# Constant products in TensorE's waits while two norms finish, and the first two weight pieces behind each norm multiplied pass by pass

## The chip, the core and the metric

The kernel runs on one NeuronCore of one Trainium2 chip. The metric is the device time of one execution in microseconds (us); lower is better. Times of whole kernels are given as the median of several executions. One execution was also taken by the hardware profiler; its rows are what the prediction reads.

## The reference

A trunk of two layers over 256 tokens of width 1024, all in float32. The lines that matter for this change are the norms with their scale and shift, and the dense matrix products right behind two of them:

```python
def rmsnorm(x, g):
    xf = x.astype(jnp.float32)
    y = xf * lax.rsqrt(jnp.mean(xf * xf, axis=-1, keepdims=True) + EPS)
    return (y * g.astype(jnp.float32)).astype(x.dtype)
...
    for l in range(DEPTH):
        if l == N_A:
            hn_kv = modulate(rmsnorm(h, kv_norm_g), kv_sh, kv_sc)
            shared = fox_shared_kv(hn_kv, fox_w_kv, fox_w_f, fox_b_f)
        a = modulate(rmsnorm(h, norm_g[l, 0]), sh1, sc1)
        if l < N_A:
            mix = retention(a, ret_w_in[l], ret_w_o[l])
        else:
            mix = forgetting_attention(a, fox_w_qg[j], fox_w_o[j], shared[0], shared[1], shared[2])
        h = h + g1[:, None, :] * mix
        m = modulate(rmsnorm(h, norm_g[l, 1]), sh2, sc2)
        if l % 2 == 0:
            ff = swiglu(m, ffn_w_gate[i], ffn_w_up[i], ffn_w_down[i])
        else:
            ff = moe_swiglu(m, router_w[i], router_b[i], moe_w_gate[i], moe_w_up[i], moe_w_down[i])
        h = h + g2[:, None, :] * ff
```

`swiglu` is `(silu(h @ w_gate) * (h @ w_up)) @ w_down` with 2816 hidden columns. `fox_shared_kv` begins with the product of the normed stream and a weight of 2048 columns, keys first. All weights together are 513 MB, read once.

## The kernel before

The residual stream `hT` is kept transposed: 8 tiles (`kt`) of 128 features by 256 tokens. The stages follow one another: retention, its output product, the dense SwiGLU, keys, values and attention, its output product, the routing and the eight experts. The first inner transition lies between the retention's output product and the SwiGLU, the second between the SwiGLU and the keys. A third one, ahead of the routing, is not touched by the change.

**Weights.** All weights come through one list of pieces of 1 MB (`stream`, L111). SyncE loads them into a ring of four raw buffers (`NR`). Each piece is used in two halves. For each half ScalarE makes a rounded copy `whi` (`act.copy`, L145) and VectorE the remainder `wlo` (L147, traced as L176), and both go into rings of six (`NW`). A product of activations and weights is three products (`PASSES`, L521): activations' high part with `whi`, high part with `wlo`, low part with `whi`. Between the weight pieces the list has pieces of the conditioning matrices, which VectorE multiplies and adds up itself (L247).

`half()` (L168) gives the caller the next half that is ready and then makes up to three more steps of the list (`fill`), as long as fewer than four halves lie ready. The ScalarE copies are issued at once; the VectorE remainders are issued after `tick()`, which moves every side job by one step (L190). In the last round ahead of a norm, `out_acc` takes its two halves with no such step (L558), so that of four ready halves two are left when the norm ends.

**The norm.** While the last round of products ends, VectorE adds each tile to `hT` (L567), ScalarE squares it (L474), and TensorE sums the squares with one-column products into `st` (L480). `Norm.finish` (L484) takes the sums that are left, then calls the first filler. By default a filler is `gap`, which turns one finished conditioning vector with eight TensorE transposes (L256). Then come the root on ScalarE (L489), some eight small VectorE steps up to the diagonal `dg` (L496), and one product `rb` that spreads the result over all partitions (L498). `modulate` (L501) makes eight scaled tiles on VectorE (`mt`, L507), their high parts on ScalarE (`mh` or `kh`, L510) and their low parts on VectorE (L513).

**Behind the norm.** `proj_b(..., first=True)` (L525) takes two halves and runs the three passes over both, tile by tile of `hT`, so that the products with the first high parts can begin before the low parts are there. The next two halves follow by the ordinary way (L533). In the SwiGLU the first two halves are the gate piece (`pg`) and the next two the up piece (`pu`); in the keys they are key pieces 0 and 1 (`pk`).

**Order.** The stages stand under a manual schedule, so that each engine takes its instructions in the order of the program. PSUM has eight banks: four of the tag "mm" (accumulators, keys) and four of the tag "at" (`st`, `rb`, transposes, `pg`, `pu`). A new tile takes the bank that was given back first in the order of the program, and its first write waits for the last reader of the tile that lay there.

Of the kernel before, what the change touches and what calls it, by code (L numbers as in the profile page):

```python
# [24 lines left out]
D, S, KT, TT = 1024, 256, 8, 2  # L25
# [30 lines left out]
def trunk(ctx: ExitStack, tc: tile.TileContext, x, c, ada_w, ada_b, norm_g, ret_w_in, ret_w_o,  # L56
# [15 lines left out]
    def bank(shape, name="pm", tag="mm"):  # L72
        return ps.tile(shape, F32, tag=tag, bufs=BANKS[tag], name=name)
# [37 lines left out]
    class Stream:  # L111
# [53 lines left out]
                steps -= 1  # L165
            return later

        def half(self, steps=3):  # L168

            while not self.made:  # L170
                self.start()
            w = self.made.pop(0)
            later = self.fill(self.spare, steps)
            tick()
            for f in later:
                f()  # L176
            return w
# [7 lines left out]
    stream = Stream()  # L185
# [4 lines left out]
    def tick():  # L190
        for g in side[::-1]:
            if next(g, "end") == "end":
                side.remove(g)
        if queue:
            g = queue.pop(0)
            if next(g, "end") != "end":
                side.append(g)
# [266 lines left out]
    class Norm:  # L464
# [16 lines left out]
                       start=(self.n == 0 and t == 0), stop=(self.n == KT - 1), skip_group_check=True)  # L481
                self.n += 1

        def finish(self, fillers=(gap, gap)):  # L484
            self.sum()
            fillers[0]()
            p = self.p
            v = self.v
            act.activation(v, self.st, AF.Sqrt, bias=epsc)  # L489
            r = p.tile([128, TT], F32, name="nr")  # L490
            u = p.tile([128, TT], F32, name="nu")
            vec.tensor_scalar(u, self.st, EPS, -0.5, op0=OP.add, op1=OP.mult)
            newton(r, u, v)
            dg = p.tile([128, TT, 128], F32, name="dg")
            for t in range(TT):
                vec.tensor_scalar(dg[:, t, :], ident, r[:, t:t + 1], None, op0=OP.mult)  # L496
            self.rb = bank([128, S], name="rb", tag="at")
            mm(self.rb, ones, dg.rearrange("p t k -> p (t k)"), start=True, stop=True)  # L498
            fillers[1]()

        def modulate(self, g, sh, hi, lo=None):  # L501

# [14 lines left out]
    def run(gen):  # L517
        for _ in gen:
            pass

    PASSES = ((0, 0), (1, 0), (0, 1))  # L521

    def proj_b(dst, xs, first=False):

        if first:  # L525
            w = [stream.half(), stream.half()]
            for i, (a, b) in enumerate(PASSES):
                for kt in range(KT):
                    for j in range(2):
                        mm(dst[:, j, :], w[j][a][:, kt, :], xs[b][:, kt, :], start=(kt + i + j == 0),  # L530
                           stop=(i == 2 and kt == KT - 1), skip_group_check=True)
            return
        for j in range(2):  # L533
            w = stream.half()
            for i, (a, b) in enumerate(PASSES):
                for kt in range(KT):
                    mm(dst[:, j, :], w[a][:, kt, :], xs[b][:, kt, :],
                       start=(kt == 0 and i == 0), stop=(kt == KT - 1 and i == 2))
# [46 lines left out]
    norm = Norm(np1)  # L585
# [29 lines left out]
    with ExitStack() as st:  # L615
# [106 lines left out]
        for h in range(RH):  # L722
            for kk in range(0, 4, 2):
                last = h == RH - 1 and kk == 2
                if last:
# [2 lines left out]
                zh, zl = zs[h]  # L728
                out_acc(acc, (zh[:, kk:kk + 2, :], zl[:, kk:kk + 2, :]), 2, h == 0 and kk == 0, last,
                        cols.get("g1_0"), norm)  # L730
        norm.finish()


    with ExitStack() as st:
        fp = st.enter_context(rpool("fp"))
        mh = fp.tile([128, KT, S], F32R, name="mh")
        ml = fp.tile([128, KT, S], F32R, name="ml")
        run(norm.modulate(gain("sc2_0", ng(1), "G01"), cols["sh2_0"], mh, ml))
        xs = (mh, ml)
        acc = accs()  # L740
        hid = []
        for j in range(NJ + 1):
            if j < NJ:
                pg = bank([128, 2, S], name="pg", tag="at")
                proj_b(pg, xs, j == 0)
                hd = fp.tile([128, 2, S], F32, tag="hd", bufs=2, name="hd")
                act.activation(hd, pg, AF.Silu)
                pu = bank([128, 2, S], name="pu", tag="at")
                proj_b(pu, xs)
                vec.tensor_tensor(hd, pu, hd, op=OP.mult)  # L750
                hh = fp.tile([128, 2, S], F32R, tag="hh", bufs=2, name="hh")
                hl = fp.tile([128, 2, S], F32R, tag="hl", bufs=2, name="hl")
                if j == 0:
                    fp.tile([128, 16], F32, name="fppad")
                split(hh, hl, hd)
                hid.append((hh, hl))
            if j:
                last = j == NJ
                if last:
                    flush()  # L760
                    norm = Norm(np1)
                out_acc(acc, hid[j - 1], 2, j == 1, last, cols.get("g2_0"), norm)
        norm.finish()


    with ExitStack() as st:
# [74 lines left out]

        kT = xp2.tile([128, KT, S], F32, name="fkT")

        def keys(j):
            pk = bank([128, 2, S], name="pk")
            proj_b(pk, kv, j == 0)
            act.copy(kT[:, 2 * j:2 * j + 2, :], pk)

        def queries(j):
            pk = bank([128, 2, S], name="pk")  # L850
# [91 lines left out]
            yield  # L942

        side.append(early())
        keys(0)
        split(wfh, wfl, wf)
        keys(1)
        keys(2)
        side.append(forget())
        keys(3)  # L950
        vv = xp2.tile([128, TT, D], F32, name="vv")
        values(0)
        values(1)
# [404 lines left out]
```

## Time and profile before

| | us |
|---|---|
| median of three executions (lowest, highest) | 1614.23 (1610.34, 1618.51) |
| profiled execution, whole | 1611.17 |
| its span, first to last instruction | 1609.4 |
| TensorE busy in the span | 1565.2 |
| VectorE busy in the span | 1403.1 |
| ScalarE busy in the span | 1104.8 |

The profiled execution is 3.06 us shorter than the median; 1.77 us of it lie outside the span. PE is TensorE's products, PEld its weight loads, DVE VectorE, ACT ScalarE, SP SyncE. A timeline line has the start, the time to the end of the last instruction of the group, the engine, the program line, the operation with its tiles and the count; in brackets stands how long the engine was idle before it and what ended that. An L480, L498 or L276 product of two float32 operands appears as two instructions. [...]

### The profile page before, as it was taken

Reading aid. Unit: us, or ns where it says so; the run is one execution under the profiler, and the core shown is the slowest. Engines: PE = TensorE matmul, PEld = TensorE weight load, DVE = VectorE, ACT = ScalarE, POOL = GpSimd, SP = SyncE. Lnnn points to the kernel's source line nnn. Section 1 sums busy time; section 2 is a strip of 40 time slices with the busy share of each in tenths; the row PEclk is TensorE's granted clock in tenths of the full one; section 3 lists DMA queues with packets and bytes.
Section 4 is the critical chain, followed back from the end, with each engine's and each line's share of the span. In section 5 each row is a group of like instructions: output and inputs, shape, how many; then the busy total and the mean of one; then the engine's idle time right before and its main releaser. Section 6 shows DMA issues by size and latency. Waiting matters only on the chain. (4 is left out here: it accounts for less than half of the span.)

```text
span 1609.4 us, 23117 instructions
## 1 busy us (share of the span) xinstructions
PE 1565.2 (97%) x8763; PEld 1350.8 (84%) x8763; DVE 1403.1 (87%) x1658; ACT 1104.8 (69%) x1531; POOL 0.2 (0%) x4
## 2 busy tenths in 40 slices
PE   5999999999999998999999999999999999999996
PEld 5888899999988886888888888888888888888884
DVE  5989887888798976989989989988989988988977
ACT  3554455544475658787888777788778787778774
POOL 0000000000000000000000000000000000000000
PEclk9999998999989998999999999999999999999999
DMA  8978786999868436999999999999999999999990
GB/s 309 333 257 312 277 317 227 340 331 365 296 235 302 140 126 253 377 372 372 357 339 363 362 374 374 361 344 367 357 381 370 356 351 361 356 387 364 359 373 27
DMA packets 182499, 516.00 MB, mean 321 GB/s; under 512 B 10320, under 2 KB 54128, under 8 KB 182384
## 3 DMA queue, kind: packets, MB, share of 16 engines
q1 hardware_dynamic: 178496, 510.82, 85.8%
q10 hardware_dynamic: 3888, 3.66, 0.7%
q8 instruction: 70, 1.15, 0.3%
q14 instruction: 45, 0.37, 0.1%
HBM read 513.40 MB, written 1.05 MB: 320 GB/s over the span
## 5 line engine op out<-in xcount | busy, mean ns | idle before, releaser
L176 DVE TENSOR_TENSOR wlo<-raw,whi 128x1024 fp32r<-128x1024 f32 x836 | 976.1, 1220 | 75.6 <-ACT whi L145 71.0
L145 ACT CAST whi<-raw 128x1024 fp32r<-128x1024 f32 x842 | 864.4, 1054 | 207.3 <-PE yd L545 56.9
L545 PE MATMUL pgu<-whi,xeh 128*128 128x512 f32 x896 | 354.2, 395 | 0.1
L545 PE MATMUL pgu<-wlo,xeh 128*128 128x512 f32 x896 | 349.6, 390 | 0.8 <-DVE wlo L176 0.8
L545 PE MATMUL pgu<-whi,xel 128*128 128x512 f32 x896 | 349.1, 390 | 0.0
L545 PEld LDWEIGHTS pgu<-whi,xel 128*128 128x128 f32 x896 | 168.3, 188 | 35.8
L545 PEld LDWEIGHTS pgu<-wlo,xeh 128*128 128x128 f32 x896 | 168.5, 188 | 33.8 <-DVE wlo L176 1.4
L545 PEld LDWEIGHTS pgu<-whi,xeh 128*128 128x128 f32 x896 | 168.4, 188 | 33.2 <-ACT whi L145 0.5
L545 PE MATMUL yd<-wlo,ehh 128*128 128x512 f32 x448 | 174.5, 390 | 1.2 <-DVE wlo L176 1.2
L545 PE MATMUL yd<-whi,ehh 128*128 128x512 f32 x448 | 174.4, 389 | 0.0
L545 PE MATMUL yd<-whi,ehl 128*128 128x512 f32 x448 | 174.3, 389 | 0.0
L247 DVE SCALAR_TENSOR_TENSOR adaacc<-raw,csil,adaacc 128x1024 f32<-128x1024 f32 x108 | 138.5, 1283 | 3.4 <-DMA raw<-in_ada_w_dram 1.3
L545 PEld LDWEIGHTS yd<-wlo,ehh 128*128 128x128 f32 x448 | 84.1, 188 | 19.4 <-DVE wlo L176 2.1
L545 PEld LDWEIGHTS yd<-whi,ehh 128*128 128x128 f32 x448 | 84.1, 188 | 17.4
L545 PEld LDWEIGHTS yd<-whi,ehl 128*128 128x128 f32 x448 | 84.1, 188 | 17.4
L205 DVE TENSOR_TENSOR ehl<-pTe,ehh 128x512 fp32r<-128x512 f32 x56 | 38.7, 691 | 37.9 <-ACT ehh L204 37.7
L1201 ACT ACTIVATE ehd<-pgu 128x512 f32<-128x512 f32 x56 | 33.5, 600 | 30.9 <-PE pgu L545 30.9
L204 ACT CAST ehh<-pTe 128x512 fp32r<-128x512 f32 x56 | 32.9, 587 | 28.2 <-PE pTe L1136 28.2
L545 PE MATMUL pa<-whi,ah 128*128 128x512 f32 x128 | 50.4, 393 | 0.0
L545 PE MATMUL pa<-whi,al 128*128 128x512 f32 x128 | 50.4, 393 | 0.0
L545 PE MATMUL pa<-wlo,ah 128*128 128x512 f32 x128 | 50.1, 392 | 0.0
L561 PE MATMUL acc<-hh,whi 128*128 128x256 f32 x176 | 49.1, 279 | 0.0
(349 smaller groups left out, 2008.9 us busy)
## 6 DMA issues: line engine op xcount, KB each, us to landing
raw<-in_moe_w_gate_dram SPq DMA_DIRECT2D x112, 1024.0 KB, 7.2
raw<-in_moe_w_up_dram SPq DMA_DIRECT2D x112, 1024.0 KB, 7.3
raw<-in_moe_w_down_dram SPq DMA_DIRECT2D x112, 1024.0 KB, 7.4
raw<-in_ada_w_dram SPq DMA_DIRECT2D x48, 1024.0 KB, 6.8
raw<-in_ret_w_in_dram SPq DMA_DIRECT2D x24, 1024.0 KB, 6.8
raw<-in_ffn_w_gate_dram SPq DMA_DIRECT2D x11, 1024.0 KB, 6.6
raw<-in_ffn_w_up_dram SPq DMA_DIRECT2D x11, 1024.0 KB, 7.0
raw<-in_ffn_w_down_dram SPq DMA_DIRECT2D x11, 1024.0 KB, 7.5
```

The lines of the kernel that those rows point to most:

```text
L145: act.copy(hi, part)
L176: f()
L204: act.copy(hi, src)
L205: vec.tensor_tensor(lo, src, hi.bitcast(F32), op=OP.subtract)
L247: vec.scalar_tensor_tensor(acc, raw[:, kt % 2, :], csil[:, kt:kt + 1], acc, op0=OP.mult, op1=OP.add)
L545: mm(dst, xs[b][:, kt0 + k, t * 128:t * 128 + 128], w[a][:, k, :], start=(first and k == 0 and i == 0), stop=(last and k == nk - 1 and i = ...
L561: mm(acc[nt // 2][:, nt % 2, :], w[a][:, k, nt % 4 * 128:nt % 4 * 128 + 128], xs[b][:, k, :], start=(first and nt % 2 == 0 and k == 0 and ...
L1201: act.activation(hd, pd, AF.Silu)
```

## The change

It has two parts, and both touch the two inner transitions alone.

First, `Norm.finish` takes `spans`, and with `SPANS = (256, 512, 512)` it issues three TensorE products of constants (identity times the constant block, float32) whose results nobody reads: one of 256 columns ahead of the remaining sums, one of 512 behind the first filler and so ahead of `rb`, one of 512 behind `rb`. Each takes a bank of the tag "mm".

Second, the first two pieces behind the norm are taken together in `proj_b2`: four halves are taken at once, the first two of them with the usual three steps, the other two with none, and all four without `tick`. Then pass 0 runs over the eight tiles with four products per tile (two into the first bank, two into the second), then pass 1, then pass 2. After pass 0 comes one `tick`, after pass 1 two, after pass 2 two. In the SwiGLU the bank of `pu` is therefore taken at the start, and the Silu of `pg` follows behind both. In the keys the split of the forget weight moves behind both pieces, and the two copies to `kT` come together.

```diff
-        def half(self, steps=3):
+        def half(self, steps=3, beside=True):
...
-            tick()
+            if beside:
+                tick()
...
-        def finish(self, fillers=(gap, gap)):
+        def finish(self, fillers=(gap, gap), spans=()):
+            if spans:
+                busy(spans[0])
             self.sum()
             fillers[0]()
+            if spans:
+                busy(spans[1])
...
             mm(self.rb, ones, dg.rearrange("p t k -> p (t k)"), start=True, stop=True)
             fillers[1]()
+            if spans:
+                busy(*spans[2:])
...
+    def busy(*ns):
+
+        for n in ns:
+            mm(bank([128, 512], name="idle")[:, 0:n], ident, cm[:, 0:n], start=True, stop=True)
+
     PASSES = ((0, 0), (1, 0), (0, 1))
+    SPANS = (256, 512, 512)
+
+    def proj_b2(dsts, xs):
+
+        w = [stream.half(3 if j < 2 else 0, False) for j in range(4)]
+        for i, (a, b) in enumerate(PASSES):
+            for kt in range(KT):
+                for j in range(4):
+                    mm(dsts[j // 2][:, j % 2, :], w[j][a][:, kt, :], xs[b][:, kt, :], start=(kt + i + j % 2 == 0),
+                       stop=(i == 2 and kt == KT - 1), skip_group_check=True)
+            tick()
+            if i:
+                tick()
...
-        norm.finish()
+        norm.finish(spans=SPANS)
...
-                proj_b(pg, xs, j == 0)
+                if j:
+                    proj_b(pg, xs)
+                else:
+                    pu = bank([128, 2, S], name="pu", tag="at")
+                    proj_b2((pg, pu), xs)
                 hd = fp.tile([128, 2, S], F32, tag="hd", bufs=2, name="hd")
                 act.activation(hd, pg, AF.Silu)
-                pu = bank([128, 2, S], name="pu", tag="at")
-                proj_b(pu, xs)
+                if j:
+                    pu = bank([128, 2, S], name="pu", tag="at")
+                    proj_b(pu, xs)
...
-        norm.finish()
+        norm.finish(spans=SPANS)
...
-        def keys(j):
-            pk = bank([128, 2, S], name="pk")
-            proj_b(pk, kv, j == 0)
-            act.copy(kT[:, 2 * j:2 * j + 2, :], pk)
+        def keys(js):
+            pks = [bank([128, 2, S], name="pk") for _ in js]
+            if len(js) == 2:
+                proj_b2(pks, kv)
+            else:
+                proj_b(pks[0], kv)
+            for j, pk in zip(js, pks):
+                act.copy(kT[:, 2 * j:2 * j + 2, :], pk)
...
-        keys(0)
+        keys((0, 1))
         split(wfh, wfl, wf)
-        keys(1)
-        keys(2)
+        keys((2,))
         side.append(forget())
-        keys(3)
+        keys((3,))
```

## Rows read from the trace of the kernel before

**Rows 1.** The profile's page, part 1 (busy time of each engine) part 2 (granted clock of TensorE in 40 equal slices of the span) and one group of part 5 (busy us, mean ns of one, idle us before).

```profile
PE 1565.2 (97%) x8763; PEld 1350.8 (84%) x8763; DVE 1403.1 (87%) x1658; ACT 1104.8 (69%) x1531; POOL 0.2 (0%) x4
...
PEclk9999998999989998999999999999999999999999
...
L176 DVE TENSOR_TENSOR wlo<-raw,whi 128x1024 fp32r<-128x1024 f32 x836 | 976.1, 1220 | 75.6 <-ACT whi L145 71.0
```

**Rows 2.** The windows of one us each in the first inner transition: busy time of PE, PEld, DVE, ACT and POOL, then the granted clock, the DMA share and GB/s.

```profile
246.00:247.00 1.00, 0.98 (x9) 0.98 (x10) 0.00 (x0) 0.36 (x1) 0.00 (x0) 1.00 0.17 61
247.00:248.00 1.00, 1.00 (x7) 1.00 (x7) 0.47 (x4) 0.26 (x1) 0.00 (x0) 0.57 0.02 6
...
257.00:258.00 1.00, 1.00 (x9) 1.00 (x9) 1.00 (x2) 0.97 (x6) 0.00 (x0) 0.81 0.03 8
```

**Rows 3.** The timeline of the first inner transition, from the last sums to the second gate piece.

```profile
246.02 1.05 PE L480 MATMUL st<-invd,sq 128*128 128x1 f32 x8 [0.24 <-ACT sq L474]
...
246.94 1.78 PE L256 MATMUL pc<-cm,adaacc 128*128 128x128 f32 x8
...
248.32 0.48 DVE L496 TENSOR_SCALAR dg<-cm,nr 128x128 f32<-128x128 f32 x2
...
248.86 1.22 PE L498 MATMUL rb<-dg,cm 128*128 128x256 f32 x2
250.12 3.22 DVE L507 SCALAR_TENSOR_TENSOR mt<-hT,G,rb 128x256 f32<-128x256 f32 x8 [1.24 <-PE rb L498]
250.63 3.32 ACT L510 ACTIVATE mh<-mt,ada_sh 128x256 fp32r<-128x256 f32 x8 [3.20 <-DVE mt L507]
...
251.19 3.79 PE L530 MATMUL pg<-mh,whi 128*128 128x256 f32 x16 [1.12 <-ACT mh L510]
...
253.86 1.98 ACT L145 CAST whi<-raw 128x1024 fp32r<-128x1024 f32 x2
...
254.78 3.21 PE L530 MATMUL pg<-mh,wlo 128*128 128x256 f32 x16
...
262.36 1.07 PE L537 MATMUL pu<-mh,whi 128*128 128x256 f32 x8
...
263.26 1.07 PE L537 MATMUL pu<-mh,wlo 128*128 128x256 f32 x8
...
265.07 1.07 PE L537 MATMUL pg<-mh,whi 128*128 128x256 f32 x8
```

**Rows 4.** The timeline of the second inner transition, from `rb` to key piece 2.

```profile
443.48 1.19 PE L498 MATMUL rb<-dg,cm 128*128 128x256 f32 x2 [0.26 <-DVE G L369]
444.71 3.23 DVE L507 SCALAR_TENSOR_TENSOR mt<-hT,Gkv,rb 128x256 f32<-128x256 f32 x8 [1.22 <-PE rb L498]
...
445.79 3.78 PE L530 MATMUL pk<-kh,whi 128*128 128x256 f32 x16 [1.11 <-ACT kh L510]
...
448.43 2.00 ACT L145 CAST whi<-raw 128x1024 fp32r<-128x1024 f32 x2
...
451.02 3.22 DVE L507 SCALAR_TENSOR_TENSOR mt<-hT,G,rb 128x256 f32<-128x256 f32 x8
...
454.23 1.04 PE L256 MATMUL pc<-cm,adaacc 128*128 128x128 f32 x8
...
455.10 1.88 PE L276 MATMUL pr<-adaacc,cm 128*128 128x512 f32 x4
...
456.42 1.49 PE L537 MATMUL pk<-kh,whi 128*128 128x256 f32 x8
...
462.27 1.07 PE L537 MATMUL pk<-kh,whi 128*128 128x256 f32 x8
```

**Rows 5.** The windows of one us each in the second inner transition, with the granted clock behind the five busy times.

```profile
441.00:442.00 1.00, 1.00 (x10) 1.00 (x10) 0.00 (x1) 0.26 (x1) 0.00 (x0) 0.85 0.00 0
...
451.00:452.00 1.00, 1.00 (x7) 1.00 (x6) 1.00 (x4) 0.94 (x7) 0.00 (x0) 0.53 0.03 12
```

**Rows 6.** The timeline of the third transition, which the change leaves alone: transposes, `rb`, the first small product behind a long wait, and the first dense products.

```profile
599.51 1.07 PE L993 MATMUL pht<-cm,hT 128*128 128x128 f32 x8
...
601.53 0.67 PE L498 MATMUL rb<-dg,cm 128*128 128x256 f32 x2 [0.95 <-DVE G L369]
...
611.64 0.27 PE L1049 MATMUL pcum<-sel,strir 128*128 128x8 f32 x1 [2.64 <-DVE sel L1045]
...
618.81 1.19 PE L1113 MATMUL pxe<-P,mth 128*128 128x256 f32 x4 [1.97 <-DVE cmax L1065]
```

**Rows 7.** The windows of 1.5 us each in the third transition, with the granted clock behind the five busy times.

```profile
600.50:602.00 1.50, 0.55 (x3) 0.44 (x3) 0.88 (x5) 0.76 (x2) 0.00 (x0) 1.00 1.02 415
...
611.00:612.50 1.50, 0.72 (x5) 0.63 (x5) 1.43 (x5) 1.50 (x3) 0.00 (x0) 0.96 0.62 243
...
621.50:623.00 1.50, 1.50 (x10) 1.50 (x10) 0.00 (x0) 1.09 (x5) 0.00 (x0) 0.63 1.02 421
```

**Rows 8.** The timeline of TensorE in the attention stage, where a product waits while others with everything at hand stand behind it.

```profile
523.05 1.10 PE L276 MATMUL pr<-adaacc,cm 128*128 128x512 f32 x2 [0.42 <-DVE dm L902]
523.59 0.68 PE L537 MATMUL pk<-qh,whi 128*128 128x256 f32 x1
```

**Rows 9.** Two long windows behind the transitions, most of the SwiGLU and most of the keys, values and attention.

```profile
270.00:430.00 160.00, 160.00 (x1414) 160.00 (x1414) 134.63 (x127) 80.95 (x145) 0.00 (x0) 1.00 0.95 342
460.00:590.00 130.00, 129.47 (x993) 113.36 (x992) 117.96 (x228) 82.79 (x180) 0.00 (x0) 1.00 0.65 226
```

## The prediction

> **What bounds the kernel now.** I read the page first: TensorE is busy for 97% of the span and its clock is full almost everywhere, with three slices below 9 tenths only where a norm lies [rows 1]. So a microsecond that TensorE loses or wins counts in full, unless something later has slack. The long windows behind the transitions show none: TensorE is busy for 160.00 of 160.00 us in the SwiGLU and 129.47 of 130.00 us from the keys to the attention [rows 9], and the waits at the routing stand behind all of it. What a transition wins or loses is therefore taken to reach the end one to one.
>
> Then I read the two transitions by window and by timeline. The reader is to see two things. First, the clock is 1.00 until the squares are summed, falls to 0.50 at about 247.1 and 441.7 and is back about 257.4 and 451.9 [rows 2, 5]. It fell while TensorE was busy 0.98 of the microsecond, with one-column sums, after an idle time of 0.24 us [rows 2, 3]. Second, ScalarE's order: the eight high parts begin at 250.63, and right behind them, at 253.86, come two casts of 1.98 us together [rows 3]; in the keys the casts begin at 448.43 [rows 4]. They make the third and fourth weight half: two halves are left when the norm ends, and the steps of the first `half()` behind it make the next two.
>
> **The change part by part.**
>
> *Unit prices.* Dense products of 256 columns at full clock: eight from 262.36 to 263.26 plus the next groups, about 0.113 each; at half clock 16 in 3.21, 0.20 each [rows 3]. A float32 product of 512 columns: two of them (four instructions) from 455.10 to 456.42, and the eight key products behind them take 1.49 instead of 1.07, so 0.42 of the two lies in there: 1.74, or 0.87 each [rows 4]; half of that, 0.43, for 256; double at half clock. `rb` takes 1.22 at half clock [rows 3] and 0.67 at full [rows 6].
>
> *The product ahead of the last sums* (0.43). The idle 0.24 us behind tile 5's sum [rows 3] hides some of it: the root comes 0.2 us later.
>
> *The product ahead of `rb`* (0.87). If the clock holds, the eight transposes take 1.04 as at 454.23 [rows 4] instead of 1.78 [rows 3]; with sums ending at 247.3, TensorE is through with both at about 249.2. The diagonal, done at 248.80 before [rows 3], is done at 249.0. So `rb` starts 0.35 later than at 248.86 and is 0.55 shorter: the scaled tiles begin 0.2 to 0.4 us earlier, and I take 0.3. The same steps from 443.48 and 444.71 [rows 4] give 0.3 too. The cover here is the chain of small VectorE steps; at half clock it doesn't suffice (second rival).
>
> *The product behind `rb`* (0.87) lies in the 1.11 us that TensorE waits for the first high part [rows 3, 4] and costs nothing; it is over before that part is there.
>
> *The four halves together.* This is the term that decides. In `proj_b2` the third product of the first tile needs the third half, and the fourth the fourth half. Their casts stand behind all eight high parts in ScalarE's queue. TensorE keeps its order: in the attention a product waits 0.42 us while others stand behind it [rows 8]. So after two products TensorE waits for the first cast and, after one more, for the second. Before, it spent that time on pass 0 and part of pass 1 of the first two halves.
>
> First transition: the casts end at 255.84 [rows 3], less 0.3 is 255.54, and with a hand-over of 0.04, as from `rb`'s end to the first scaled tile, the fourth product starts at 255.58. From it to the first product of the next piece are 93 steps of 0.1132 (0.9057 for eight), 10.53: 266.11, against 265.07 now [rows 3]. **+1.0 us at full clock.** The bank of `pu` is that of `rb`; its last reader, the eighth scaled tile, ends at 253.34 [rows 3] and is earlier than the cast. The bank costs nothing here; it would cost if the casts were there in time (third rival).
>
> Second transition: casts end at 450.43 [rows 4], less 0.3, plus 0.04: 450.17; plus 10.53; plus the transposes and the two spreads that side jobs put between the passes, 456.42 less 454.23 and the 0.42 from above, 2.61 [rows 4]: 463.31, against 462.27. **+1.0 us at full clock.** Here the side jobs bring a wait: the eight scaled tiles of the queries (3.22 us [rows 4]) read `rb`'s bank. They now stand behind pass 0's tick, so behind the remainders of four halves and two additions on VectorE, and one of the four banks for transposes and spreads is `rb`'s. From the end of the low parts at 451.02 [rows 4], less 0.3, four remainders of 1.22 [rows 1] and two additions of about 1 each bring VectorE to 457.6, and it ends the tiles at 460.8; TensorE at full clock wants the last bank at about 458.5, at half clock 2 us later. Bounds 0 and 2.2; I take 0.4, near the lower end, because the clock makes TensorE late.
>
> *The clock in the new wait.* TensorE has two, then one product between about 250.9 and 255.6, some 4.6 us. The trace does not show such a wait here; the nearest row is the third transition, where an idle time of 2.64 us up to 611.64 and small products behind it ended in a fall at about 612.4 [rows 6, 7]. So I take it that the clock falls. How long do dense products then run at half? In the third transition 618.81 to about 622.6, 3.8 us [rows 6, 7]; in the first two from 251.19 to 257.4 and from 445.79 to 451.9, 6.2 us [rows 2 to 5]. By 0.20 against 0.113 that is 19 products and 1.6 us, or 31 and 2.7 us. I take 2.2, between them, as the two rows are equally near. Lower end 0: it doesn't fall. **+2.2 us in each transition.**
>
> *The ticks* (five for four), the later Silu and the two later copies lie on ScalarE and VectorE beside 5 us of products from the two halves that are still ready, and cost nothing; if that cover is gone, a cast and a remainder, 1.0 and 1.2 us, would show. SyncE's loads start with the remainders: the first two raw buffers come free about as now, the next ones up to 3 us later, and TensorE wants their data some 3 us later too.
>
> *Sum:* 1.0 + 1.0 + 2 x 2.2 + 0.4 = **+6.8 us**. On the profiled execution 1611.17 becomes 1618.0. The median stands 3.06 higher, and I forecast for it: 1614.23 + 6.8 = 1621.0.
>
> [...] Between the constant products stand eight transposes, and in the third transition the clock was 1.00 through eight transposes at 599.51, an idle time of 0.95, `rb` and eight more [rows 6, 7]. [...] The measurement is on the side of holding.
>
> **The rivals.**
>
> *The clock survives the new wait* (or is back ahead of the fourth product). For it: the third transition kept 1.00 through several short gaps [rows 7]. Against it: 4.6 us is longer than the gap that ended in a fall. Then the sum is 1.0 + 1.0 + 0.4 = 2.4: 1616.6.
>
> *The clock falls ahead of `rb`* (slower than before by more than can be mistaken). The place: the transposes, the 512-column product, then `rb` in one queue. At half clock from 247.3: transposes 1.78, product 1.74, `rb` 1.22 end at 252.0, so the scaled tiles begin 1.9 later than at 250.12, which is 2.2 later than in the forecast. One transition gives 6.8 + 2.2 = 9.0, 1623.2; both give 11.2, 1625.4. It decides from the point where 0.43 us of constant columns is too little to hold the clock that fell at 247.1. For it: the same stretch lost the clock twice. Against it: the third transition's similar stretch didn't.
>
> *The four halves are at hand* (the change does what it is for). First transition: two products at 250.9, the third when `rb`'s bank is free, 253.34 less 0.3; 94 steps later it is 263.7, so 1.4 us won. Second: from 445.5, 96 steps and 2.61 give 459.0, 3.3 us won. Together -4.7: 1609.5. Against it: both pairs of casts stand behind the high parts now, and nothing in the change puts them ahead.
>
> **How the numbers follow.** Forecast 0.64 (1621.0; its own range 1619.4 to 1623.8, from 1.6 and no bank wait to 2.7 and 2.2 for the bank); clock survives 0.10 (1616.6); clock falls ahead of `rb` in one or both 0.22 (1623.2 to 1625.4); halves at hand 0.04 (1609.5). The range reaches from 1611 to 1628: the three executions here spread by 4 us to either side of their median, so it takes in the middle of every case but the last, whose 1609.5 lies outside. About 0.5%, 8.07 us, is what a measurement of this kernel can tell from no change. Slower by more: all of the second rival but a little, 0.20, and a fifth of the forecast, 0.13: 0.33. Faster by more: 0.02, if the third rival wins more than its sum. Within: 0.65.
>
> **What would show it.** In the changed trace: `rb` near 0.7 and the scaled tiles some 0.3 us earlier (if they are 2 us later, the clock fell first). On TensorE two products, then an idle time of about 3.5 us ended by ScalarE's cast, one product, another idle 0.9; then a dense run whose first 4 to 6 us have the clock 0.50. The first product of the second gate piece about 3.2 us later than now, that of key piece 2 about 6.8 us later. I am wrong if the third product follows the second without a wait for `whi`; then the third rival holds. The size is wrong if the clock is 1.00 in the dense run, or if TensorE waits behind `proj_b2` for weights or for a bank.

## The result

| | us, median (lowest to highest) | executions |
|---|---|---|
| before | 1612.17 (1608.71 to 1618.51) | 11 |
| after | 1621.78 (1620.83 to 1624.36) | 11 |
| ratio | 1.0064, interval 1.0054 to 1.0074 | |

The change makes the kernel slower by some 10 us, just over the 0.5% that can be told from no change. The time of after is that of the forecast, 1621.0, but part of this is luck: on more executions before stands 2 us lower than the 1614.23 that the forecast started from, and the loss is 3 us larger than the 6.8 of the sum. To a loss beyond the 0.5% the prediction had given a chance of 0.33, to a change within it 0.65.

To compare traces I measure from one event, the start of the last two squares ahead of each norm, to the end of the first two weight pieces behind it ("the pair"; in the keys with the transposes and spreads that lie between), and from the same event to that of the next norm. A pair ends where the next instruction behind it starts. Before, by the first two lines here, the squares start at 245.55 and 440.09, and by [rows 3, 4] the pairs end at 265.07 and 462.27; after, by the other two, the squares start at 246.36 and 446.01:

```profile
245.55 0.81 ACT L474 ACTIVATE sq<-hT 128x256 f32<-128x256 f32 x2 [1.47 <-DVE hT L567]
440.09 0.81 ACT L474 ACTIVATE sq<-hT 128x256 f32<-128x256 f32 x2 [1.47 <-DVE hT L567]
...
246.36 0.81 ACT L475 ACTIVATE sq<-hT 128x256 f32<-128x256 f32 x2 [1.47 <-DVE hT L592]
446.01 0.81 ACT L475 ACTIVATE sq<-hT 128x256 f32<-128x256 f32 x2 [1.47 <-DVE hT L592]
```

The page of after (span 1620.6, the execution 1622.37), its parts 1 and 2, beside [rows 1]:

```profile
PE 1570.9 (97%) x8775; PEld 1353.7 (84%) x8775; DVE 1403.5 (87%) x1658; ACT 1104.3 (68%) x1531; POOL 0.2 (0%) x4
...
PEclk9999999999999997999999999999999999999998
```

TensorE has 12 instructions more, six products of two, and 5.7 us more busy time. Of the three low slices of [rows 1] only that of the third transition is left; the slices of the two inner transitions have a mean clock of 0.96 (243.1 to 283.6) and 0.92 (445.7 to 486.2), print as 9 and hold a fall each, so a slice at 9 doesn't mean that the clock held. The timeline of TensorE in the first transition, the lines that answer to [rows 3]:

```profile
246.51 1.40 PE L481 MATMUL st<-invd,sq 128*128 128x1 f32 x12
247.77 1.07 PE L257 MATMUL pc<-cm,adaacc 128*128 128x128 f32 x8
248.68 1.02 PE L531 MATMUL idle<-cm 128*128 128x512 f32 x2
249.69 0.70 PE L503 MATMUL rb<-dg,cm 128*128 128x256 f32 x2
250.23 1.02 PE L531 MATMUL idle<-cm 128*128 128x512 f32 x2
...
251.50 0.50 PE L542 MATMUL pg<-mh,whi 128*128 128x256 f32 x2 [0.26 <-ACT mh L517]
...
255.23 0.38 PE L542 MATMUL pu<-mh,whi 128*128 128x256 f32 x1 [3.23 <-DVE ml L520]
256.18 0.58 PE L542 MATMUL pu<-mh,whi 128*128 128x256 f32 x1 [0.56 <-ACT whi L145]
...
268.36 1.03 PE L257 MATMUL pc<-cm,adaacc 128*128 128x128 f32 x8
...
270.62 1.21 PE L562 MATMUL pg<-mh,whi 128*128 128x256 f32 x8 [1.22 <-ACT pc L262]
```

The reader is to see: `rb` at 0.70 and not 1.22, so the clock held; two products, then 3.23 us of nothing, one product, 0.56 of nothing; a dense run to 268.36; and a second wait of 1.22 behind it. The line names VectorE's `ml` for the first wait, but that is only what ended last by the profile: VectorE's low parts have no part in pass 0. ScalarE's timeline shows the cast that it waits for, and what comes later:

```profile
250.94 3.30 ACT L517 ACTIVATE mh<-mt,ada_sh 128x256 fp32r<-128x256 f32 x8 [2.67 <-DVE mt L514]
254.15 3.87 ACT L145 CAST whi<-raw 128x1024 fp32r<-128x1024 f32 x4
...
269.00 0.26 ACT L262 ACTIVATE pc<-pc 128x128 f32<-128x128 f32 x1 [8.02 <-PE pc L257]
...
272.05 1.28 ACT L776 ACT_TABLE_LOAD   x1
273.34 0.60 ACT L776 ACTIVATE hd<-pg 128x512 f32<-128x512 f32 x1
...
275.22 3.90 ACT L145 CAST whi<-raw 128x1024 fp32r<-128x1024 f32 x4
```

ScalarE then stands idle for 8.02 us, because its next instructions in order read transposes that a tick has put behind pass 2, and the Silu and the next casts stand behind those. The windows of one us (length, TensorE's busy time, its granted clock as a share of the full one, DMA share, GB/s) place the fall at 256.0, at the end of the wait of 0.56: the product at 255.23 still took 0.38, that at 256.18 took 0.58:

```profile
255.00:256.00 1.00, 0.38 (x1) 1.00 0.00 0
256.00:257.00 1.00, 0.82 (x4) 0.52 0.00 0
...
259.00:260.00 1.00, 1.00 (x9) 0.77 0.03 8
```

The second transition, to set against [rows 4]:

```profile
449.44 0.67 PE L503 MATMUL rb<-dg,cm 128*128 128x256 f32 x2
...
451.23 0.51 PE L542 MATMUL pk<-kh,whi 128*128 128x256 f32 x2 [0.26 <-ACT kh L517]
454.95 0.58 PE L542 MATMUL pk<-kh,whi 128*128 128x256 f32 x1 [3.22 <-ACT whi L145]
455.90 5.88 PE L542 MATMUL pk<-kh,whi 128*128 128x256 f32 x29 [0.37 <-ACT whi L145]
461.62 3.79 PE L542 MATMUL pk<-kh,wlo 128*128 128x256 f32 x32
465.25 1.03 PE L257 MATMUL pc<-cm,adaacc 128*128 128x128 f32 x8
466.13 1.88 PE L277 MATMUL pr<-adaacc,cm 128*128 128x512 f32 x4
...
471.62 1.10 PE L562 MATMUL pk<-kh,whi 128*128 128x256 f32 x8
```

Where the time went (us; most of the kernels that follow in the same columns, each from the trace of one execution; in the row of jobs earlier the eight transposes that lie inside its first pair, 0.79, are taken off):

| kernel | last squares to end of first pair | norm 1 to norm 2 | last squares to end of second pair | norm 2 to norm 3 |
|---|---|---|---|---|
| before | 19.52 | 194.54 | 22.18 | 158.04 |
| after | 22.00 | 199.65 | 25.61 | 161.53 |
| products only | 17.36 | - | - | - |
| passes only | 23.37 | 200.60 | 26.38 | 162.59 |
| casts ahead | 19.84 | 198.14 | 27.49 | 163.40 |
| clock held | 20.51 | 198.16 | 26.21 | 162.02 |
| passes in the SwiGLU only | 23.16 | 201.18 | 20.15 | 155.98 |
| halves made early | 16.57 | 198.55 | 30.38 | 166.31 |
| jobs earlier | 22.04 | 197.04 | 24.85 | 160.97 |
| two products | 20.24 | 196.44 | 21.16 | 157.16 |
| fed, transposes late | 16.15 | 191.38 | 21.52 | 157.27 |

By this table after loses 2.48 in the first pair, 2.63 more on the way to norm 2 (5.11 in all), 3.43 in the second pair and 0.06 behind it. The rest of the 11.2 us between the two spans (0.81 ahead of norm 1, 1.79 behind norm 3) lies where the two kernels are the same; behind norm 3 the other kernels stand between 0.8 less and 1.9 more than before.

### The profile page after: what moved, and what is told of

Read it like the earlier page. It is cut to its first block, busy times and chain, and to the rows that moved or that the text cites. A ratio compares the mean times of both kernels' runs of the same rounds, so it can differ in the third digit from the quotient of the medians.

```text
span 1620.6 us, 23145 instructions
## 1 busy us (share of the span) xinstructions
PE 1570.9 (97%) x8775; PEld 1353.7 (84%) x8775; DVE 1403.5 (87%) x1658; ACT 1104.3 (68%) x1531; POOL 0.2 (0%) x4
```

## The experiments

**The two parts apart.** Products only: the pass order of before, `proj_b(pg, xs, j == 0)` and `keys((0,))`, with the spans kept.

> The constant products stay in both transitions, the pass order behind them is that of the kernel before (two halves, then two). Theory A (the loss is the wait for the casts of the third and fourth half and the fall of the clock in that wait; the constant products by themselves win): the spread is 0.7 instead of 1.2 us, the clock stays at 1.00 through the first two halves, which end about 2 us earlier in each transition: 4.3 us in all, ratio to the kernel before 0.9973. Theory B (the constant products cost: the one ahead of the spread holds it up, and the extra clock gives nothing back): ratio 1.000 to 1.003.

Measured: 1607.88, ratio 0.9979 (0.9968 to 0.9990). The products alone win. The profile fell on its longest execution (1619.23), in which TensorE waited 3.20 us ahead of the second norm and the clock was at half from some 435 to 452 us (mean 0.76, 0.50 and 0.89 in the ten us from 430, 440 and 450), so only its first transition is read. TensorE's timeline there: the products start with the first high part, no wait for a half follows, and the pair, from squares at 245.17, ends at 262.52.

```profile
250.32 3.30 PE L555 MATMUL pg<-mh,whi 128*128 128x256 f32 x16 [0.26 <-ACT mh L517]
...
262.52 1.07 PE L562 MATMUL pg<-mh,whi 128*128 128x256 f32 x8
```

Passes only, the other way round:

```diff
-        norm.finish(spans=SPANS)
+        norm.finish()
...
```

> No constant products; the four halves are taken together as in the changed kernel. Theory A: TensorE still waits 3 us and 0.6 us for the two casts, the dense run starts 0.3 us later than in the changed kernel and at half clock; the up piece's end and key piece 1's end come 3 to 4 us later than in the kernel before, and 1 to 2 us follow behind the first transition (bank and remainders): 8 to 11 us in all, ratio 1.005 to 1.007. Theory B: without the constant products the pass order is neutral, ratio 1.000 to 1.002.

Measured: 1621.70, ratio 1.0068 (1.0054 to 1.0082). So the loss is the passes', 3.85 and 4.20 us in the pairs. Ahead of the passes the products win 1.37 and 0.77 us of the pairs, where they win 2.16 and 2.03 alone, and in the time of the whole nothing of it is seen (1.0068 without them, 1.0064 with them).

**The casts.** The third and fourth half are cast right behind the norm's root, where ScalarE idles; their remainders run at the start of `proj_b2`, that is behind the low parts.

```diff
             act.activation(v, self.st, AF.Sqrt, bias=epsc)
+            self.later = stream.fill(stream.spare, 2) if spans else []
...
```

> The changed kernel with one thing moved: the two ScalarE casts of the third and fourth half are issued right behind the norm's root, in ScalarE's idle time ahead of the high parts; their remainders follow on VectorE behind the low parts. Theory A: no wait for a cast is left. In the first transition TensorE then waits for the spread's bank (about 2 us), 1.4 us won there, some of it given back behind it; in the second 3.3 us won. Ratio to the kernel before 0.997 to 0.999. Theory C (the loss is that four halves held at once starve what follows): the wait for the casts goes, but the time behind the pieces grows by as much; ratio 1.003 to 1.006.

Measured: 1622.87, ratio 1.0077 (1.0064 to 1.0091), a miss. The wait for the casts is gone and others stand in its place. In the first transition TensorE waits 1.70 for `rb`'s bank, then twice for a remainder, 0.41 and 0.75:

```profile
252.77 0.50 PE L545 MATMUL pu<-mh,whi 128*128 128x256 f32 x2 [1.70 <-DVE mt L515]
...
258.21 0.38 PE L545 MATMUL pu<-mh,wlo 128*128 128x256 f32 x1 [0.75 <-DVE wlo L540]
...
455.27 0.38 PE L545 MATMUL pk<-kh,wlo 128*128 128x256 f32 x1 [2.36 <-DVE wlo L540]
...
466.31 1.12 PE L277 MATMUL pr<-adaacc,cm 128*128 128x512 f32 x2 [1.80 <-DVE mt L515]
```

In the second, 2.36 for a remainder and 1.80 at the spread, whose bank the queries' scaled tiles still read. The clock fell right behind the first of these waits (0.89 from 454 to 456 and 0.50 from 456, so at half from some 455.6), and that pair ends 1.88 later than with the casts late.

**The clock.** Constant products fill part of the wait:

```diff
+                    if i + kt == 0 and j == 2:
+                        busy(512, 512, 512)
...
```

> The changed kernel with three more constant products of 512 columns between the second and the third product of pass 0, in the wait for the first cast (2.6 us of work in 3.2 us of waiting); the accumulators of the SwiGLU are taken after the first round so that a bank is free for them. Theory A: the clock stays at 1.00 in the dense run, which takes 10.5 us instead of 12.2 in each transition: 3.3 us less than the changed kernel, ratio to the kernel before 1.004. If the clock had no share in the loss, the ratio stays at 1.006.

Measured: 1620.13, ratio 1.0062 (1.0048 to 1.0076), short of the 1.004 of A; from the 1.0064 of after it can't be told. In the first transition it does what it should: the clock holds (two products take 0.39 or 0.40 from 254.98 on, where after has 0.63 from 256.56) and the pair ends 1.49 earlier. In the second it fell ahead of `rb`, in the transposes, and then TensorE, early again, waited for the spread's bank:

```profile
444.50 1.85 PE L257 MATMUL pc<-cm,adaacc 128*128 128x128 f32 x8
446.15 1.92 PE L531 MATMUL idle<-cm 128*128 128x512 f32 x2
...
464.69 1.13 PE L277 MATMUL pr<-adaacc,cm 128*128 128x512 f32 x2 [1.41 <-DVE mt L514]
```

**Which transition.** Passes in the SwiGLU alone; the keys go as before, with the products.

> Both pairs of constant products stay; only the SwiGLU's first two pieces are taken together, key pieces 0 and 1 go in the order of before. Theory A (each transition carries its own loss: the passes lost 3.43 us in the second transition against before, and the products alone should win about 1.2 there): 1.0064 less 4.6 of 1612 us, ratio 1.0035 (1.002 to 1.005). Rival B (what is lost is lost once, in the weight halves that run dry behind the first transition, and the second only shows it later): ratio 1.005 to 1.0065. Rival C (nearly all is lost in the keys): 0.999 to 1.001. In the profile by A: key piece 0's first 48 products start 4.9 us behind the last squares at full clock and no wait for whi stands there.

Measured: 1616.12, ratio 1.0050 (1.0031 to 1.0068), between the bounds of A and B. The trace decides for A: the second pair, from squares at 445.62, ends 20.15 behind them, 2.03 better than before and 5.46 better than after.

```profile
465.77 1.07 PE L562 MATMUL pk<-kh,whi 128*128 128x256 f32 x8
```

**Halves made early.** `w = stream.half(ahead if last else 3)` with `ahead=1` in the last output product, `pu` in a bank of the other tag.

> The change, but the last output product of each inner transition takes one step of the stream at each of its two halves (before: none), so that the third and fourth half and their remainders are cast before the norm ends; and the up piece's bank is one of the other four, so that it is not that of the broadcast. Theory A (the passes lose only because their third and fourth half are not there): no wait for whi, wlo or a bank inside the passes, the first two pieces end about 16 us behind the last squares in the first transition (after: 22.0, products alone: 17.4), and the whole is faster than before: ratio 0.9965 to 0.9985. Rival B (the passes lose by themselves: four halves held to the end of pass 2 starve what follows): the pair ends early, but the next pieces wait, ratio 0.999 to 1.003. Rival C (casts between the squares delay the norm): the last squares come over 1 us later against the last output product, ratio over 1.003.

Measured: 1627.09, ratio 1.0097 (1.0073 to 1.0122). The first pair is as fast as expected, 16.57, but four things eat it. The casts between the squares put the last squares themselves at 248.33, 2 to 4 us later than elsewhere. Behind the pair TensorE waits 1.46 for a half. Ahead of the second norm it waits 1.44 for squares, and the clock is at half from some 440 to 454 us (mean 0.52 and 0.80 in the ten us from 440 and 450). And in the keys, with both passes done early, the spread waits 6 us for its bank:

```profile
470.82 2.08 PE L277 MATMUL pr<-adaacc,cm 128*128 128x512 f32 x2 [5.99 <-DVE mt L514]
```

VectorE's own timeline says why: the queries' tiles stand behind two remainders and three additions (the first of them just ahead of these lines).

```profile
462.76 2.35 DVE L177 TENSOR_TENSOR wlo<-raw,whi 128x1024 fp32r<-128x1024 f32 x2
465.04 2.60 DVE L248 SCALAR_TENSOR_TENSOR adaacc<-raw,csil,adaacc 128x1024 f32<-128x1024 f32 x2
467.55 3.22 DVE L514 SCALAR_TENSOR_TENSOR mt<-hT,G,rb 128x256 f32<-128x256 f32 x8
```

**The wait behind the passes.** The same change with the SwiGLU's ticks 2, 3, 0 for 1, 2, 2.

> The change, but in the SwiGLU's first two pieces the five ticks lie 2, 3, 0 behind the passes instead of 1, 2, 2, so that the eight transposes and ScalarE's readings of them come between pass 1 and pass 2 and no longer between pass 2 and the first Silu. Theory A (that order is what makes the second gate piece wait 1.22 us): the wait is gone, the Silu comes 3 us earlier, 1.2 to 2 us less than the change: ratio 1.0052 to 1.0057. Rival B (the second gate piece then waits for something else that is as late, a weight half): ratio 1.006 to 1.007, and the wait stands there with another name.

Measured: 1619.04, ratio 1.0055 (1.0038 to 1.0071). Without the transposes the first pair still takes 22.04, but the way from norm 1 to norm 2 is 2.61 shorter: all of the 2.63 that lay behind the pair. TensorE waits for nothing there (busy for 10.00 of every 10 us from 260 to 440), and the Silu, from squares at 246.13, runs 23.3 behind them and not 27.0. In the time of the whole the gain is not clear of noise: the interval overlaps that of after.

```profile
269.43 0.60 ACT L775 ACTIVATE hd<-pg 128x512 f32<-128x512 f32 x1
```

**More slots.** Eight slots for halves during the SwiGLU: `hir.extend(fx, 2, "ffn")`, the same for `lor`.

> The change, with two more slots for high halves and two for remainders during the SwiGLU (8 for 6), nothing else. Theory A (behind the passes TensorE waits for halves because four of six slots are held to the end of pass 2, while ScalarE idles for 8 us): two more casts are made ahead of it, the waits at the first and second up pieces behind (276 and 293 us) go, 0.8 to 1.4 us less than the change: ratio 1.0055 to 1.006. Rival B (the loads are what is late, not the slots): ratio 1.0064 and the same waits.

Measured: 1631.90, ratio 1.0132 (1.0115 to 1.0149), a miss, and no answer to its question: the two slots also moved the side jobs, and a group of transposes came ahead of the additions that it reads; the clock fell as that wait ended.

```profile
300.38 1.94 PE L257 MATMUL pc<-cm,adaacc 128*128 128x128 f32 x8 [3.78 <-DVE adaacc L248]
...
328.85 1.10 PE L562 MATMUL pg<-mh,wlo 128*128 128x256 f32 x8
329.79 1.11 PE L562 MATMUL pg<-ml,whi 128*128 128x256 f32 x8
```

Besides, eight products take 0.94 here and not 0.906 as in [rows 3], at clock 1.00, over most of the SwiGLU (last section).

**Feeding the passes.** Casts behind the root; remainders between the scaled tiles and the low parts; pass 1 half by half; `pu` in the other tag; ticks moved; in the keys the queries' tiles ahead.

```diff
+            for f in self.later:
+                f()
...
-            for kt in range(KT):
-                for j in range(4):
+            for n in range(4 * KT):
+                j, kt = (n // KT, n % KT) if i == 1 else (n % 4, n // 4)
...
```

> The change with all that its passes waited for put right. The third and fourth half are cast behind the norm's root, their remainders stand on VectorE between the scaled tiles and the low parts; pass 1 goes half by half; the up piece's bank is not the broadcast's; in the SwiGLU the ticks lie 2, 3, 0, in the keys 1, 0, 4 behind the passes, and the queries' scaled tiles are issued ahead of the keys. Theory A (fed passes win what the high parts' pace leaves beside the constant products, some 1 us in each transition): the pair ends 16.5 us behind the last squares in the first transition and 19 in the second (before 19.5 and 22.2, products alone 17.4 and 20.2), ratio 0.9955 to 0.9975. Rival B (VectorE's longer row behind the norm decides in the keys, the spread waits for the queries' tiles again): the first transition as in A, a wait of 1 us or more at the spread, ratio 0.998 to 1.002. Rival C (four held slots starve what follows in both): the pairs end early and TensorE waits for whi behind them, ratio over 1.000.

> As the kernel with everything put right, but only in the SwiGLU; key pieces 0 and 1 go in the order of before, with the constant products. Theory A: the first transition's pair ends 16.5 us behind the last squares, nothing waits behind it, the second transition is that of the products alone: ratio 0.9965 to 0.998, at or a little under the products alone (0.9979). Rival C (four held slots starve what follows): pair early, 1 to 3 us of waits for whi in the next two pieces, ratio 0.998 to 1.001.

Measured: 1613.30, ratio 1.0014 (1.0001 to 1.0026) in both transitions; 1611.70, ratio 1.0001 (0.9991 to 1.0010) in the first alone. No half and no remainder is waited for, and a bank only in the keys of the kernel with both, 0.8 us for two spreads. Yet both miss A: the ticks that helped a late TensorE now put the transposes 2.62 us ahead of VectorE's additions, and the clock fell in the transposes behind that wait (first transition alone, 1.31 for the eight) or right behind them (both); in the kernel with both it also fell ahead of the second `rb` (1.80 for the eight transposes there). From that kernel, the first transition:

```profile
261.61 1.09 PE L257 MATMUL pc<-cm,adaacc 128*128 128x128 f32 x8 [2.62 <-DVE adaacc L248]
262.46 0.61 PE L546 MATMUL pg<-ml,whi 128*128 128x256 f32 x2
```

The same, first transition alone, ticks 1, 1, 0, so that the transposes lie in the middle of the second gate piece, as before the change:

> As the kernel whose SwiGLU alone takes its first two pieces together and is fed, but with the ticks 1, 1, 0 behind the passes instead of 2, 3, 0: the side job's eight transposes then come where they did before the change, in the middle of the second gate piece, and no longer 2.6 us ahead of VectorE's additions that they read. Theory A (with halves, remainders, bank and transposes all in time the passes lose nothing and win the pace of the high parts, 0.8 us beside the products alone): pair ends 16.6 us behind the last squares (before 19.5, products alone 17.4), no wait up to the third gate piece, ratio 0.9965 to 0.9985. Rival C (four of six slots held to the end of pass 2 starve the second up piece): pair as in A, then a wait of 1 to 2 us for whi or wlo, ratio 0.998 to 1.0005.

Measured: 1606.88 (before beside it 1610.59), ratio 0.9982 (0.9968 to 0.9996). The passes run dense from the first high part to the next piece:

```profile
250.38 0.51 PE L546 MATMUL pg<-mh,whi 128*128 128x256 f32 x2 [0.26 <-ACT mh L521]
...
254.13 1.98 PE L546 MATMUL pg<-mh,wlo 128*128 128x256 f32 x16
255.94 1.98 PE L546 MATMUL pu<-mh,wlo 128*128 128x256 f32 x16
...
261.38 1.07 PE L565 MATMUL pg<-mh,whi 128*128 128x256 f32 x8
```

The pair, from squares at 245.23, ends 16.15 behind them: 3.37 better than before, 5.85 better than after, 1.21 better than the products alone (in the table: fed, transposes late). From there to 300 us TensorE waits for nothing (busy for 10.00 of every 10 us from 260), so the four slots held to the end of pass 2 starve nothing here, which is the question that the eight slots left open. Against the products alone the whole is no faster than can be told (0.9982 and 0.9979); in the profiled execution its second transition lost the clock ahead of `rb` (0.58 from 438 to 439, then 0.50), and its pair there is 21.52 and not 20.15. Both beat before.

**The third product.** Products only, `SPANS = (256, 512)`.

> The pass order of before with two constant products: the one ahead of the last sums and the one ahead of the broadcast; the third, behind the broadcast, is left out. Theory A (the third lies in an idle time that the clock stands anyway): broadcast 0.70 and first products at full clock, ratio as with three products, 0.997 to 0.999. Theory B (it is the third that holds the clock until the first high part): the clock falls behind the broadcast and the first 16 to 31 products run at half, ratio 0.9985 to 1.0005.

Measured: 1609.80, ratio 0.9993 (0.9980 to 1.0007), in the range of B; its interval overlaps that of three products. The second transition shows B by itself: the broadcast at full clock (0.67), then half clock (0.50 from 448 to 451):

```profile
446.46 3.68 PE L555 MATMUL pk<-kh,whi 128*128 128x256 f32 x16 [1.12 <-ACT kh L517]
449.94 2.55 PE L555 MATMUL pk<-kh,wlo 128*128 128x256 f32 x16
```

From the first key product to the transposes that follow the first piece are 7.69 us (446.46 to 454.15), against 6.79 with the third product in the keys' old order (450.83 to 457.62, passes in the SwiGLU only): the fall costs 0.9. In the first transition the clock fell already ahead of `rb` (1.86 for the transposes), was full again at the first product (1.00 from 250 to 253), and fell once more behind it, from some 253 to 256.5 (mean 0.83 from 250 to 260).

## Why the prediction was right, and where it was not

**What bounds the kernel.** Right: TensorE's losses reach the end. 5.11 and 3.49 us at the two norms make 8.6 of the some 10; the rest isn't explained.

**The products.** `rb` took 0.70 and 0.67, the third product cost nothing. But it is not idle: left out, the clock falls behind the broadcast and 0.9 us are lost, which the step, that saw only its price, did not say. What the prediction never priced is the products by themselves: they win 2.16 and 2.03 us in the pairs. A sum with the parts apart would have shown that the passes cost 4.64 and 5.46 there, and that the 4.2 which the products win alone hide part of these 10.1.

**The halves come late.** Right in mechanism and size. Predicted: the fourth product 10.03 behind the squares (255.58 against 245.55), measured 9.82; in the keys 10.08, measured 9.89. Casts ahead removes exactly this wait. The "halves at hand" rival would have given 1.4 us in the first pair; fed, it gives 3.37 with the products' share. But that case needs more than the rival said: remainders, a bank and the transposes too, as the waits of the runs above show.

**The clock in the new wait.** It fell, 1.65 us in the first pair (93 products from 256.18 to 268.36 are 12.18 against 10.53); 2.2 was taken, from 1.6 to 2.7. One execution doesn't fix this size: the same products take 1.68, 2.08 and 2.80 us more than 10.53 in the traces of jobs earlier, eight slots and passes in the SwiGLU only. Held by constant products the first pair ends 1.49 earlier, which shows that it is the clock. In the second pair the same sum leaves about 2.6 us (15.72 from the fourth product, less 10.53 and 2.61), of which the slower step of 0.118 in its third pass has some 0.1 (last section).

**The bank in the keys.** Nothing, where 0.4 was taken between 0 and 2.2: TensorE, at half clock, came late enough. The mechanism was right: 1.41 us when the clock is held, 1.80 with the casts ahead, 5.99 with halves and remainders ahead, beyond the bound, which had TensorE wait for the halves first.

**What failed: the ticks, the later Silu and the later copies at no cost.** They cost 2.63 us behind the first pair, for which the sum had zero. The cover that was named, products of the two halves still ready, was there, but the step looked only for VectorE's remainder and a cast. It missed the order on ScalarE: the last tick puts eight readings of transposes between pass 2 and the Silu, ScalarE idles 8.02 us ahead of them, and the Silu comes 3.7 us later than with the jobs earlier. The second gate piece waits 1.22 for its bank, and the halves behind it are late. Such a wait for a bank behind `proj_b2` the prediction had named as a sign that its size is wrong. Jobs earlier takes 2.61 of the 2.63 back. With 2.48 + 2.63 + 3.43 the sum would have been 8.5 and not 6.8.

**The rivals.** The clock fell ahead of `rb` in neither transition of the profiled execution of after, so the forecast's case held. But it is a real case: of 22 profiled transitions with the product ahead of `rb` and with the clock full ahead of the sums, it fell there in four (as in the rows of the clock held), each time putting `rb` 1.3 to 1.5 us later. What separates the four, whose eight transposes took 1.80 to 1.86, from the other eighteen, where they took 1.07, stays open: the instructions ahead are the same, and with passes only eight transposes took 1.07 at the second norm with no product ahead of them, and the clock fell only behind them (`rb` took 1.19). Before, both falls lie in the transposes too, and not in the sums, as the prediction read them: by [rows 2, 5] the clock fell at 247.14 and 441.70, and the transposes start at 246.94 [rows 3] and here:

```profile
441.47 1.75 PE L256 MATMUL pc<-cm,adaacc 128*128 128x128 f32 x8
```

## What to carry to other kernels

Work that lets an engine go on earlier is worth only what its next inputs allow: taken together, two pieces need four cast halves, four remainders, a bank and side jobs in time, and each one mended alone left or moved a wait. Price the parts of a change apart, above all where one wins and one loses, and follow every queue to the next instruction of the same engine that others wait for. Fill an idle time of TensorE with constant products where the trace shows its clock fall; here three small ones at each of two norms won 3.3 us of 1611.

## What was not expected of the hardware

Dense products of 128x256 have more than one step at granted clock 1.00: 0.113 us (0.906 for eight, [rows 3]) and 0.118 (0.94, the two lines of the eight-slot kernel above), in places 0.120 (0.96 for eight, from 287.86 to 293.62 in the same kernel). A stretch keeps one of them for many products. In two places the step is another behind something that comes between: in after it is 0.118 from 471.62 to the forget gate's products at 477.3 and 0.113 behind them (from 480.02), and in the eight-slot kernel eight transposes at 422.49 stand between 0.118 and 0.113. But eight transposes at 330.74 there left it at 0.118. That kernel has 0.118 or more from 280 to 296, and from 318 on 86 to 88 products in each ten us up to 420, where before has 90 or 91; by these counts some 5 us in all, an estimate. The rows don't show what sets the step; loads ran in some of these stretches and not in others (DMA share in after 0.01 from 471.62 to 477.28, in the eight-slot kernel 0.94 from 320 to 330, both at 0.118 or more).
